# Feed-forward shift and scale as TensorE blocks in the state-space layer, weight remainders there on VectorE, lent buffers returned early

## The chip, the cores and the metric

The kernel runs on one core of one Trainium2 chip. The metric is device time in microseconds (us) of one execution, the median of three runs. In the profile PE is TensorE (PEld its weight loads), DVE is VectorE, ACT is ScalarE, POOL is GpSimd and SP is the queue that issues the DMAs. Each engine works through its own instructions in their order and waits at an instruction until its inputs are there and its output buffer is free.

## The reference, cut to what matters

The whole is four transformer-like layers over 256 tokens of width 1024, in float32. The change lies in one of them, the second layer of the first block: a state-space mixer (S5) with a gate, whose two neighbours are feed-forwards.

```python
def modulation(cs, w, b):
    m = cs @ w + b
    shift, scale, gate = jnp.split(m, 3, axis=-1)
    return shift[:, None, :], scale[:, None, :], gate[:, None, :]

def s5_mixer(h, w_in, ..., w_glu, b_glu, w_out):
    u = h @ w_in
    ...                               # bu = u times B, a scan over time, y = C times the state + d * u
    g = jax.nn.gelu(y)
    z = g * jax.nn.sigmoid(g @ w_glu + b_glu)
    return z @ w_out

    # in layer i, with cs = silu(c), c of shape (1, 1024):
    x = layer_norm(ALPHA * x + (1.0 + gate) * y, ln_mix_g[i], ln_mix_b[i])
    shift, scale, gate = modulation(cs, mod_ffn_w[i], mod_ffn_b[i])
    h = x * (1.0 + scale) + shift
```

A modulation is a product of one row of 1024 with a 1024 x 3072 matrix: little arithmetic, 12 MB of weights. The second feed-forward's shift and scale (`mod30` and `mod31` in the kernel) are needed at the end of the state-space layer.

## The kernel before, in words

All weights come as units of 128 x 1024 float32 (512 KB). `plan()` puts the units into one order, SP loads them in that order into seven buffers `raw`, and `run(maxn)` processes the next units, at most `maxn`, where the program calls it. A buffer is loaded again when its unit has been processed.

A weight unit (`"w"`) is split into a rounded part and a remainder, so that three products of the faster float32r kind give a float32 result. ACT writes the rounded part `wh` (L454). The remainder `wl` is written by DVE in one instruction (L460), or, for the units listed in `POOLED`, by POOL in four of 256 columns (L458). Both go to one of 11 slots (`RING`), and the slot is free again when the matmuls that read it have been issued. Three of the 11 slots (`SPARE`) are lent to the state-space layer, which keeps its operators in them (`self.rt`), so in that layer only eight slots are there for weights: the eight units `ssm_glu` of the gate fill them.

A modulation unit (`"m"`) holds 128 rows of a transposed weight matrix; DVE multiplies it with `cs`, which is spread over the partitions, and sums each row (L508, with a short second instruction that reads the sum). Eight units make the 1024 values of a third (shift, scale or gate), and one small addition of the bias (L517) ends it.

The state-space layer is written by hand as a string of steps, `SSM_SEQ`. Ahead of them stands a pass of the input projection: for each half of the tokens and each of two column blocks n, 8 units of `ssm_in` by three matmuls of 512 columns, with `run` after each unit as `FRUN` says, and a 32 x 32 block transposition on DVE (L1545) after each column block. The last of these passes is the one of half 1, n = 1. In the string the letters with a block number 0 to 3 mean:

- V: enter, 16 float32 matmuls of 64 columns on PE
- R: rotate, four products on DVE (L1571 to L1575), two sums on POOL (L1573, L1576)
- S: scan, two scans and four products on DVE (L1585 to L1591), two sums on POOL (L1589, L1592)
- O: put out, 24 float32 matmuls of 128 columns on PE, then copies by ACT (L1610)
- U: eight transposes on PE (L1620), then the gelu on ACT and DVE, and the split of its result
- G: gates, 48 float32r matmuls of 256 columns on PE; G0 needs all of `ssm_glu`
- X and W expand operators on ACT; a bare number is `run(maxn=number)`

A float32 matmul stands as two records in the trace, each with a weight load of its own. After G3 come the sigmoid by tanh, the split of the gated values into `hh` and `hl` in four blocks of two rows of 128 (L1657 to L1662), with `run(maxn=2)` after each, and then the output projection `ssm_out`: two passes over 8 units, one for each half of the tokens, the first of which needs blocks in their order. The layer norm follows (L651 and on).

What sets the order of work is thus the text of the program: nothing is moved by a scheduler, and each engine's queue is the order in which the steps were called.

Of the kernel before, what the change touches and what calls it, by code (L numbers as in the profile page):

```python
# [15 lines left out]
OP = mybir.AluOpType  # L16
# [16 lines left out]
LATE = {'mla_o': 3, 'mlp0.d': 6, 'ssm_out': 3, 'mlp1.d': 3, 'f10.d': 2, 'lru_out': 2, 'f20.d': 2, 'f11.d': 1, 'att_o': 1, 'f21.d': 3}  # L33
LATE_F = {"mlp0.f": 2, "ssm_in": 2, "mlp1.f": 2, "f10.f": 2, "lru_x": 2, "f20.f": 2, "kv_v": 2, "f11.f": 2, "att_q": 2, "f21.f": 2}
SSM_PRE = 2
SSM_SEQ = "V0 R0 V1 2 X2 0 0 S0 R1 1 V2 X3 W0 4 S1 R2 1 0 2 O0 W1 V3 U0 1 R3 1 S2 1 1 O1 W2 U1 G0 1 S3 W3 O2 1 0 0 0 G1 3 U2 2 O3 U3 0 19 2 1 G2 13 G3"
LRU_SEQ = "X0 X1 C0 X2 C1 Y0 R0 C2 R1 D0 X3 I0 9 I1 C3 Y1 G0 1 G1 7 1 Y2 D1 I2 R2 D2 Y3 I3 R3 G2 G3 D3 A0 1 Q2 3 4 Q1 Q0 6 M0 T0 A1 Q3 M1 A3 3 A2 L0 T1 M2 L1 T2 M3 T3 L2 L3 3 5"
LRU_POOL = {'A0', 'D0', 'D3', 'L2', 'M0', 'M1', 'M2', 'M3', 'N1', 'P0', 'P1', 'P2'}
HEADS0 = "T2 S0 B0 1 A2 E0 N0 t q t 1"
# [42 lines left out]
    return out  # L82


POOLED = {('att_o', 4), ('att_o', 6), ('att_q', 2), ('att_q', 4), ('f20.f', 3), ('f20.f', 6), ('f21.f', 2), ('f21.f', 4), ('f21.f', 7), ('lru_i', 0), ('lru_out', 0), ('lru_out', 1), ('lru_out', 2), ('lru_out', 3), ('lru_out', 4), ('lru_r', 1), ('lru_x', 7), ('lru_y', 2), ('mlp0.f', 3), ('mlp0.f', 4), ('mlp0.f', 5), ('mlp0.f', 7), ('mlp1.f', 1), ('mlp1.f', 2), ('mlp1.f', 3), ('mlp1.f', 4), ('mlp1.f', 5), ('mlp1.f', 6), ('ssm_glu', 1), ('ssm_glu', 2), ('ssm_glu', 3), ('ssm_glu', 4), ('ssm_glu', 5), ('ssm_glu', 6), ('ssm_glu', 7), ('ssm_out', 0), ('ssm_out', 1), ('ssm_out', 2), ('ssm_out', 4)}
LRU_W = _w("lru_x", 8) + _w("lru_y", 2) + [("w", "lru_r", 0), ("w", "lru_i", 0)] + _w("lru_y", 6)[2:]
LRU_W += [("w", "lru_r", 1), ("w", "lru_i", 1)] + _w("lru_y", 8)[6:] + _w("lru_out", 8)
MODS0 = _mod(2, 0) + _mod(2, 1) + _mod(1, 2)
MODS_AT = 8
MODS_PRE = 7  # L90
ON = 1
OM = 4
MM = 3
# [32 lines left out]
def _unit(inp, kind, tag, k, out):  # L126
    def rows(w, cols=slice(0, 1024)):
        out[:] = w[128 * k:128 * k + 128, cols]

    def col(w):  # L130
        out[:] = w[:, 128 * k:128 * k + 128].reshape(8, 128, 128).transpose(1, 0, 2).reshape(128, 1024)

    if kind == "m":
        i, third = int(tag[3]), int(tag[4])
        nm, l = _MOD[i]
        o = 1024 * third + 128 * k
        out[:] = inp[nm + "_w"][l][:, o:o + 128].T
        return
    if tag[:3] in _FFN:
        nm, l = _FFN[tag[:3]]  # L140
        g, u, d = (inp["%s_w_%s_2" % (nm, s)][l] for s in ("gate", "up", "down"))
        part = tag[4]
        if part == "f":
            out[:, :512] = g[128 * k:128 * k + 128, :512]
            out[:, 512:] = u[128 * k:128 * k + 128, :512]
        elif part == "d":
            rows(d)
        else:
            col(g if part == "g" else u)
        return  # L150
    if tag[:3] == "mlp":
        w1, w2 = inp["mlp_w1"][int(tag[3])], inp["mlp_w2"][int(tag[3])]
        if tag[5] == "u":
            col(w1)
        else:
            rows(w1 if tag[5] == "f" else w2)
        return
    if tag == "mla_in":
        w = inp["mla_w_in"][0][256 * k:256 * k + 256].reshape(2, 128, 448)
        out[:, :896] = w.transpose(1, 0, 2).reshape(128, 896)  # L160
    elif tag in ("kvk", "kvv"):
        w = inp["mla_w_kvb"][0].reshape(128, 8, 2, 128)
        out[:] = w[:, :, 0 if tag == "kvk" else 1].reshape(128, 1024)
    elif tag == "qb":
        w = inp["mla_w_qb"][0].reshape(2, 128, 8, 192)[:, :, 2 * k:2 * k + 2]
        o = out.reshape(128, 2, 4, 128)
        for s in range(2):
            o[:, s, 0:2] = w[s, :, :, :128]
            o[:, s, 2] = w[s, :, :, 128:].reshape(128, 128)
            sw = np.concatenate([w[s, :, :, 160:], w[s, :, :, 128:160]], axis=-1)  # L170
            o[:, s, 3] = sw.reshape(128, 128)
    elif tag == "mla_o":
        rows(inp["mla_w_o"][0])
    elif tag == "ssm_in":
        rows(inp["ssm_w_in"][0])
    elif tag == "ssm_glu":
        col(inp["ssm_w_glu"][0])
    elif tag == "ssm_out":
        rows(inp["ssm_w_out"][0])
    elif tag == "lru_x":  # L180
        rows(inp["lru_w_in_2"][0])
    elif tag == "lru_y":
        col(inp["lru_w_in_2"][0][:, 1024:])
    elif tag in ("lru_r", "lru_i"):
        w = inp["lru_w_%s_2" % tag[4]][0][2 * k:2 * k + 2].reshape(2, 2, 128, 256)
        out[:] = w.transpose(2, 0, 1, 3).reshape(128, 1024)
    elif tag == "lru_out":
        rows(inp["lru_w_out_2"][0])
    elif tag == "kv_v":
        rows(inp["w_kv_2"], slice(1024, 2048))  # L190
    elif tag == "kv_k":
        col(inp["w_kv_2"])
    elif tag == "att_q":
        rows(inp["attn_w_q_2"][0])
    elif tag == "att_o":
        rows(inp["attn_w_o_2"][0])
    else:
        raise KeyError(tag)


def _cols_spec():
    s = [("dsk", lambda i: i["ssm_d"][0])]
    for m, (nm, l) in _MOD.items():
        s.append(("modb%d" % m, lambda i, nm=nm, l=l: i[nm + "_b"][l]))
    for nm in ("ln_mix", "ln_ffn"):
        for l in range(2):
            for gb in "gb":
                key = "%s_%s" % (nm, gb)
                s.append((key + str(l), lambda i, key=key, l=l: i[key][l]))
# [12 lines left out]
    return s
# [92 lines left out]
class Model:  # L315
    def __init__(self, ctx, tc, ws, cols, rows, x, pos, inv, rel, sp, sbc, sgb, out):
# [181 lines left out]
    def mod_unit(self, u, raw):  # L498
        nc, tag, k = self.nc, u[1], u[2]
        i, third = int(tag[3]), int(tag[4])  # L500
        if k == 0:
            self.mod_finish()
        total = (self.gcol if tag == "mod01" else self.msum)[:, k:k + 1]
# [421 lines left out]
    def setup(self):  # L925
# [572 lines left out]
    def ssm(self, begin):  # L1498
# [68 lines left out]
        def rotate(b):  # L1567
# [2 lines left out]
            c, sn = tabs[b][:, 0:512], tabs[b][:, 512:1024]  # L1570
            V.tensor_tensor(t[0], vr, c, op=mul)  # L1571
            V.tensor_tensor(t[1], vi, sn, op=mul)
            nc.gpsimd.tensor_tensor(t[0], t[0], t[1], op=add)  # L1573
            V.tensor_tensor(t[2], vi, c, op=mul)
            V.tensor_tensor(t[3], vr, sn, op=mul)  # L1575
            nc.gpsimd.tensor_tensor(t[2], t[2], t[3], op=sub)  # L1576
            self.rel(vr, vi)

        def scan(b):
# [6 lines left out]
            V.tensor_tensor_scan(t[3], mkb, t[2], 0.0, op0=mul, op1=add)  # L1586
            V.tensor_tensor(t[0], t[1], c, op=mul)
            V.tensor_tensor(t[2], t[3], sn, op=mul)
            nc.gpsimd.tensor_tensor(sh(xr)[:, :, 1:64], sh(t[0])[:, :, 0:63], sh(t[2])[:, :, 0:63], op=sub)  # L1589
            V.tensor_tensor(t[1], t[1], sn, op=mul)  # L1590
            V.tensor_tensor(t[3], t[3], c, op=mul)  # L1591
            nc.gpsimd.tensor_tensor(sh(xi)[:, :, 1:64], sh(t[1])[:, :, 0:63], sh(t[3])[:, :, 0:63], op=add)  # L1592
            if b == 0:
                nc.sync.dma_start(out=tabs[3], in_=self.tab_d[3])
            if b == 3:
# [45 lines left out]
                        self.done(u)  # L1641

        for step in SSM_SEQ.split():
            f = {"X": lambda b: expand("g", b), "W": lambda b: expand("h", b), "V": enter, "R": rotate, "S": scan, "O": put_out, "U": unit, "G": gates}.get(step[0])
            if f:
                f(int(step[1:]))
            else:
                self.run(maxn=int(step), mods=99)
        self.rt = []
        self.hidden(1)  # L1650
        bh = self.stat(8)
        V.tensor_scalar(bh, self.col("bglu", 0, 8), 0.5, None, op0=mul)
# [368 lines left out]
```

## Time and profile before

| | |
|---|---|
| median of three runs | 1743.57 us (1743.54 to 1747.07) |
| profiled execution | 1742.75 us, span 1740.9 us |
| PE busy | 1602.5 us (92% of the span) |
| DVE, ACT, POOL busy | 67%, 48%, 29% |
| mean granted TensorE clock | 0.956 of full |

The time of an execution lies 1.85 us above the span of its profile. PE is busy for nearly all of the span; the stretch from about 421 to 505 us, the steps V2 to G3 of the state-space layer, is one of the places where it is not. A share of busy time over the whole span says little of this stretch, so it is read by itself below, with the pass ahead of it (from 400 us) and the gated tail behind it (to 528 us).

### The profile page before, as it was taken

Reading aid. Unit: us, or ns where it says so; the run is one execution under the profiler, and the core shown is the slowest. Engines: PE = TensorE matmul, PEld = TensorE weight load, DVE = VectorE, ACT = ScalarE, POOL = GpSimd, SP = SyncE. Lnnn points to the kernel's source line nnn. Section 1 sums busy time; section 2 is a strip of 40 time slices with the busy share of each in tenths; the row PEclk is TensorE's granted clock in tenths of the full one; section 3 lists DMA queues with packets and bytes.
Section 4 is the critical chain, followed back from the end, with each engine's and each line's share of the span. In section 5 each row is a group of like instructions: output and inputs, shape, how many; then the busy total and the mean of one; then the engine's idle time right before and its main releaser. Section 6 shows DMA issues by size and latency. Waiting matters only on the chain. (4 is left out here: it accounts for less than half of the span.)

```text
span 1740.9 us, 25278 instructions
## 1 busy us (share of the span) xinstructions
PE 1602.5 (92%) x9690; PEld 1417.2 (81%) x9690; DVE 1157.7 (67%) x1480; ACT 833.7 (48%) x1252; POOL 508.8 (29%) x557
## 2 busy tenths in 40 slices
PE   4778999998789999999999759999999999999998
PEld 2557798887677899789998747999899999779997
DVE  6688986578978655776556787555656554765553
ACT  2343656555345655354445735444544443754441
POOL 8945699608848100100004441000000001230000
PEclk9869999898889999999999879999999999999999
DMA  9477678767556666466554336565455664536640
GB/s 365 172 279 256 226 248 281 273 243 263 220 170 222 239 229 212 152 219 225 176 181 134 118 121 217 176 239 173 137 188 214 213 211 133 182 133 207 214 149 25
DMA packets 106588, 349.64 MB, mean 201 GB/s; under 512 B 12385, under 2 KB 22753, under 8 KB 106466
## 3 DMA queue, kind: packets, MB, share of 16 engines
q1 hardware_dynamic: 106466, 348.02, 57.7%
q8 instruction: 76, 1.25, 0.3%
q14 instruction: 46, 0.38, 0.1%
HBM read 338.40 MB, written 9.57 MB: 200 GB/s over the span
## 5 line engine op out<-in xcount | busy, mean ns | idle before, releaser
L460 DVE TENSOR_TENSOR wl<-raw,wh 128x1024 fp32r<-128x1024 f32 x445 | 562.7, 1298 | 193.1 <-ACT wh L454 191.7
L454 ACT ACTIVATE wh<-raw 128x1024 fp32r<-128x1024 f32 x484 | 490.3, 1051 | 275.1 <-PE bank L392 140.9
L392 PE MATMUL bank<-xh,wh 128*128 128x256 f32 x1728 | 490.1, 284 | 0.0
L392 PE MATMUL bank<-xh,wl 128*128 128x256 f32 x1728 | 489.7, 283 | 0.0
L392 PE MATMUL bank<-xl,wh 128*128 128x256 f32 x1728 | 489.1, 283 | 0.0
L392 PEld LDWEIGHTS bank<-xh,wh 128*128 128x128 f32 x1728 | 330.6, 191 | 2.4 <-issue 0.2
L392 PEld LDWEIGHTS bank<-xl,wh 128*128 128x128 f32 x1728 | 330.5, 191 | 2.1
L392 PEld LDWEIGHTS bank<-xh,wl 128*128 128x128 f32 x1728 | 330.5, 191 | 0.0
L392 PE MATMUL bank<-wh,hh 128*128 128x512 f32 x736 | 297.4, 404 | 24.8 <-ACT hh L1827 23.8
L392 PE MATMUL bank<-wl,hh 128*128 128x512 f32 x736 | 294.5, 400 | 2.8 <-POOL wl L458 2.8
L392 PE MATMUL bank<-wh,hl 128*128 128x512 f32 x736 | 244.8, 398 | 4.2 <-DVE hl L590 2.0
L635 POOL TENSOR_TENSOR st<-st,mhalf 128x1 f32<-128x1 f32 (+1 forms) x33 | 21.9, 664 | 694.8 <-DVE st L643 608.1
L458 POOL TENSOR_TENSOR wl<-raw,wh 128x256 fp32r<-128x256 f32 x156 | 156.7, 1037 | 138.0 <-ACT wh L454 129.8
L392 PEld LDWEIGHTS bank<-wh,hh 128*128 128x128 f32 x736 | 142.0, 193 | 55.9 <-ACT hh L1827 25.3
L392 PEld LDWEIGHTS bank<-wh,hl 128*128 128x128 f32 x736 | 141.1, 192 | 37.5 <-DVE hl L590 2.9
L392 PEld LDWEIGHTS bank<-wl,hh 128*128 128x128 f32 x736 | 142.2, 193 | 33.1 <-POOL wl L458 5.0
L508 DVE SCALAR_TENSOR_TENSOR junk<-raw,cs 128x1024 bf16<-128x1024 f32 x96 | 138.0, 1437 | 18.3 <-DMA raw<-in_ws_dram 17.1
L392 PE MATMUL bank<-wl,xh 128*128 128x512 f32 x320 | 126.6, 396 | 1.9 <-DVE wl L460 1.0
L392 PE MATMUL bank<-wh,xh 128*128 128x512 f32 x320 | 127.4, 398 | 0.7 <-ACT wh L454 0.7
L590 DVE TENSOR_TENSOR hl<-z,hh 128x512 fp32r<-128x512 f32 x72 | 52.5, 731 | 95.5 <-ACT hh L589 95.3
L392 PE MATMUL bank<-wh,xl 128*128 128x512 f32 x320 | 102.0, 396 | 6.5 <-DVE xl L590 6.4
L589 ACT ACTIVATE hh<-z 128x512 fp32r<-128x512 f32 x72 | 45.5, 632 | 116.4 <-DVE z L875 104.4
(389 smaller groups left out, 1807.2 us busy)
## 6 DMA issues: line engine op xcount, KB each, us to landing
raw<-in_ws_dram SPq DMA_DIRECT2D x580, 512.0 KB
early<-in_ws_dram SPq DMA_DIRECT2D x10, 512.0 KB
grow<-in_rows_dram SPq DMA_DIRECT2D x9, 512.0 KB
brow<-in_rows_dram SPq DMA_DIRECT2D x6, 512.0 KB
ophh<-ops_d SPq DMA_DIRECT2D x6, 512.0 KB
ophl<-ops_d SPq DMA_DIRECT2D x6, 512.0 KB
gate<-in_rows_dram SPq DMA_DIRECT2D x5, 512.0 KB
tab_d<-early SPq DMA_DIRECT2D x4, 512.0 KB
```

The lines of the kernel that those rows point to most:

```text
L392: self.nc.tensor.matmul(out, l, r, start=start, stop=stop)
L454: self.nc.scalar.activation(self.Hs[s], raw, func=AF.Copy)
L458: self.nc.gpsimd.tensor_tensor(self.Ls[s][:, w], raw[:, w], self.f32(self.Hs[s])[:, w], op=OP.subtract)
L460: self.nc.vector.tensor_tensor(self.Ls[s], raw, self.f32(self.Hs[s]), op=OP.subtract)
L508: nc.vector.scalar_tensor_tensor(self.junk, raw, 1.0, self.cs, op0=OP.mult, op1=OP.mult, accum_out=total)
L589: self.nc.scalar.activation(hdst, src, func=AF.Copy)
L590: self.nc.vector.tensor_tensor(ldst, src, self.f32(hdst), op=OP.subtract)
L635: self.nc.gpsimd.tensor_tensor(r, v, self.mhalf[:, 0:n], op=OP.pow)
```

## The change

1. The 16 units of `mod30` and `mod31` (`ROWMODS`) are laid out as plain rows of the weight matrix. Instead of the DVE product, `pe_unit` issues eight float32 matmuls: a 128 x 128 piece of the unit is the stationary operand, one column of `cst` (the 1024 values of `cs`, laid over 128 partitions and 8 columns) is what moves, and the result is one column of a PSUM bank. All eight units add into eight columns of one bank, which is held from the first to the last; then DVE adds the bias, reading from PSUM.
2. `cst` is made at the start: one ACT and two DVE instructions on 128 x 8 values.
3. Seven units of `ssm_glu` and `ssm_out` 0, 1 and 2 leave `POOLED`: DVE writes their remainders.
4. A step Z empties `self.rt` after O3, so the three lent slots are open to weights; `SSM_W` brings `ssm_out` 0 to 2 ahead of the last two units of `mod22`, and `SSM_SEQ` processes them before G2.
5. The sums of R and S on POOL are each written in two halves.

```diff
-SSM_SEQ = "... G1 3 U2 2 O3 U3 0 19 2 1 G2 13 G3"
+SSM_SEQ = "... G1 3 U2 2 O3 Z0 U3 0 3 G2 13 G3"
-POOLED = {..., ('ssm_glu', 1), ..., ('ssm_glu', 7), ('ssm_out', 0), ('ssm_out', 1), ('ssm_out', 2), ('ssm_out', 4)}
+POOLED = {..., ('ssm_out', 4)}
+ROWMODS = {'mod30', 'mod31'}
-SSM_W = _w('ssm_glu', 8)[:4] + _mod(3, 0) + _w('ssm_glu', 8)[4:] + _mod(3, 1) + _mod(2, 2) + _w('ssm_out', 8)
+SSM_W = _w('ssm_glu', 8)[:4] + _mod(3, 0) + _w('ssm_glu', 8)[4:] + _mod(3, 1) + _mod(2, 2)[:6] + _w('ssm_out', 8)[:3]
+SSM_W += _mod(2, 2)[6:] + _w('ssm_out', 8)[3:]
...
+    def pe_unit(self, tag, k, raw):
+        nc = self.nc
+        if k == 0:
+            self.pbk = self.bank()
+        for j in range(8):
+            self.mm(self.pbk[:, j:j + 1], raw[:, 128 * j:128 * j + 128], self.cst[:, k:k + 1],
+                    k == 0 and j == 0, k == 7 and j == 7)
+        if k == 7:
+            i, third = int(tag[3]), int(tag[4])
+            dst = self.mcol[i][third] if third < 2 else self.gcol
+            nc.vector.tensor_tensor(dst, self.pbk[:, 0:8], self.col("modb%d" % i, 8 * third, 8), op=OP.add)
+            self.rel(self.pbk)
+            self.pbk = None
...
+        ct = self.col("c", 0, 8)
+        nc.scalar.activation(self.cst, ct, func=AF.Tanh, scale=0.5)
+        V.scalar_tensor_tensor(self.cst, self.cst, 1.0, ct, op0=OP.add, op1=OP.mult)
+        V.tensor_scalar(self.cst, self.cst, 0.5, None, op0=OP.mult)
...
-            nc.gpsimd.tensor_tensor(t[0], t[0], t[1], op=add)
+            for w in (slice(0, 256), slice(256, 512)):
+                nc.gpsimd.tensor_tensor(t[0][:, w], t[0][:, w], t[1][:, w], op=add)
...
-        self.rt = []
```

How the queues move. First PE, in the last pass of the input projection (half 1, n = 1), around its fifth unit; `wh` and `wl` are a unit's two parts, `xh` and `xl` those of the input. Before:

```order
L392 MATMUL bank_124<-wh_59_928,xl 128x512
L392 MATMUL bank_124<-wh_60_933,xh 128x512
L392 MATMUL bank_124<-wl_60_934,xh 128x512
L392 MATMUL bank_124<-wh_60_933,xl 128x512
L392 MATMUL bank_124<-wh_50_797,xh 128x512
L392 MATMUL bank_124<-wl_50_798,xh 128x512
L392 MATMUL bank_124<-wh_50_797,xl 128x512
L392 MATMUL bank_124<-wh_51_811,xh 128x512
```

and now:

```order
L399 MATMUL bank_125<-wh_59_932,xl 128x512
L399 MATMUL bank_129<-cst,raw_64 128x1 x8
L399 MATMUL bank_125<-wh_60_937,xh 128x512
L399 MATMUL bank_125<-wl_60_938,xh 128x512
L399 MATMUL bank_125<-wh_60_937,xl 128x512
L399 MATMUL bank_125<-wh_50_801,xh 128x512
L399 MATMUL bank_125<-wl_50_802,xh 128x512
L399 MATMUL bank_125<-wh_50_801,xl 128x512
L399 MATMUL bank_129<-cst,raw_65 128x1 x8
L399 MATMUL bank_129<-cst,raw_66 128x1 x8
L399 MATMUL bank_125<-wh_51_815,xh 128x512
```

Three modulation units stand between the units of the pass here, and a fourth before its last unit. Then PE where V1 ends and V2 begins (`z` is the projected input, `oph` and `opl` are expanded operators). Before:

```order
L392 MATMUL bank_125<-z_99,oph_2876 128x64
L392 MATMUL bank_126<-z_99,opl_2877 128x64
L392 MATMUL bank_131<-z_99,oph_2878 128x64
L392 MATMUL bank_127<-z_99,opl_2879 128x64
L392 MATMUL bank_131<-z_99,oph_2878 128x64
```

and now:

```order
L399 MATMUL bank_127<-z_99,oph_2880 128x64
L399 MATMUL bank_132<-z_99,opl_2881 128x64
L399 MATMUL bank_129<-cst,raw_68 128x1 x8
L399 MATMUL bank_129<-cst,raw_69 128x1 x8
L399 MATMUL bank_129<-cst,raw_63 128x1 x8
L399 MATMUL bank_128<-z_99,oph_2882 128x64
L399 MATMUL bank_130<-z_99,opl_2883 128x64
L399 MATMUL bank_128<-z_99,oph_2882 128x64
```

Three units stand between V1 and V2; three more follow V2, four U0, one G0 and one O2. Last DVE from the end of R1 to the start of S1 (`mc` is the finished shift, `grow` holds the rotation's table). Before:

```order
L1575 TENSOR_TENSOR z_98<-bank_125,grow 128x512
L508 SCALAR_TENSOR_TENSOR junk,msum<-raw_63,cs 128x1024
L508 SCALAR_TENSOR_TENSOR junk,msum<-raw_64,cs 128x1024
L517 TENSOR_TENSOR mc_115<-msum,cols 128x8
L1585 SCALAR_TENSOR_TENSOR z_98<-z_100,z_98 128x512
```

and now:

```order
L1610 TENSOR_TENSOR z_98<-bank_127,grow 128x512
L545 TENSOR_TENSOR mc_115<-bank_129,cols 128x8
L467 TENSOR_TENSOR wl_60_938<-raw_65,wh_60_937 128x1024
L467 TENSOR_TENSOR wl_50_802<-raw_66,wh_50_801 128x1024
L467 TENSOR_TENSOR wl_51_816<-raw_67,wh_51_815 128x1024
L1621 SCALAR_TENSOR_TENSOR z_98<-z_100,z_98 128x512
```

Two modulation products have gone from between R1 and S1, three remainders have come, and the addition of the bias now reads the PSUM bank that PE fills.

## Rows read from the trace of the kernel before

**Rows 1.** Busy time of each engine by stretch; PEclk is the granted clock.

```profile
core 0: us, PE busy (x) PEld busy (x) DVE busy (x) ACT busy (x) POOL busy (x), PEclk, DMA share, GB/s
421.20:505.35 84.15, 65.97 (x481) 62.40 (x481) 76.52 (x98) 28.37 (x56) 48.21 (x39) 0.82 0.62 221
505.35:528.26 22.91, 17.99 (x66) 13.22 (x65) 14.91 (x16) 15.91 (x23) 18.36 (x20) 0.78 0.52 179
```

**Rows 2.** Waits of PE, 421.20 to 505.35 us: total, times, longest.

```profile
PE bank L392 <- POOL ophh L1589: 7.8, 1, 7.8
PE bank L1620 <- ACT b2row L1610: 2.3, 2, 1.9
```

**Rows 3.** DVE by line, 408.6 to 503.1 us: count, busy us, mean ns.

```profile
L508 DVE SCALAR_TENSOR_TENSOR junk<-raw,cs 128x1024 bf16<-128x1024 f32 x24 | 36.1, 1504 | 3.8 <-DMA raw<-in_ws_dram 3.4
```

**Rows 4.** The page's costliest groups: DVE's remainders over the whole span.

```profile
L460 DVE TENSOR_TENSOR wl<-raw,wh 128x1024 fp32r<-128x1024 f32 x445 | 562.7, 1298 | 193.1 <-ACT wh L454 191.7
```

**Rows 5.** PE in time order (start, length): last pass, V0, V1, V2.

```profile
406.62 0.39 PE L392 MATMUL bank<-wh,xh 128*128 128x512 f32 x1
...
412.14 0.33 PE L392 MATMUL bank<-z,oph 128*128 128x64 f32 x2
...
419.01 0.39 PE L392 MATMUL bank<-z,opl 128*128 128x64 f32 x2
421.20 0.66 PE L392 MATMUL bank<-z,oph 128*128 128x64 f32 x2 [1.80 <-DVE z L1545]
...
427.62 0.64 PE L392 MATMUL bank<-z,opl 128*128 128x64 f32 x2
```

**Rows 6.** DVE in time order: the fourth modulation unit and the last transposition.

```profile
418.68 1.73 DVE L508 SCALAR_TENSOR_TENSOR junk<-raw,cs 128x1024 bf16<-128x1024 f32 x1 [3.36 <-DMA raw<-in_ws_dram]
...
420.35 0.70 DVE L1545 STREAM_TRANSPOSE z<-bank 128x512 f32<-128x512 f32 x1
```

**Rows 7.** PE in time order: first and last row of O at full clock.

```profile
485.51 0.43 PE L392 MATMUL bank<-ophl,z 128*64 128x128 f32 x2
...
490.62 0.38 PE L392 MATMUL bank<-opl,ophl 128*64 128x128 f32 x2
```

**Rows 8.** Busy time by stretch: V2 and idling, most of O0, G0.

```profile
421.20:434.66 13.46, 8.84 (x38) 7.92 (x39) 13.43 (x18) 4.17 (x7) 8.23 (x12) 0.50 0.80 292
434.66:438.36 3.70, 3.70 (x19) 3.70 (x19) 3.67 (x4) 0.97 (x2) 3.70 (x3) 0.52 0.78 282
...
462.96:468.70 5.74, 5.74 (x48) 5.69 (x48) 5.74 (x5) 3.17 (x8) 5.05 (x4) 1.00 0.74 276
```

**Rows 9.** PE in time order: a matmul of 32 columns, and what follows it.

```profile
259.63 0.31 PE L392 MATMUL bank<-z 128*128 128x32 f32 x2
259.78 0.69 PE L392 MATMUL bank<-z,b2row 128*128 128x128 f32 x4
```

**Rows 10.** Weight loads (PEld) in time order at that place.

```profile
259.52 0.30 PEld L392 LDWEIGHTS bank<-z 128*128 128x128 f32 x2
259.75 0.53 PEld L392 LDWEIGHTS bank<-z,b2row 128*128 128x128 f32 x4
```

**Rows 11.** PE in time order: tail, with 512-column matmuls at half clock.

```profile
511.69 0.63 PE L392 MATMUL bank<-wh,hh 128*128 128x512 f32 x1
512.12 0.65 PE L392 MATMUL bank<-wl,hh 128*128 128x512 f32 x1
```

**Rows 12.** Waits of PE, 505.35 to 530 us: total, times, longest.

```profile
PE bank L392 <- POOL wl L458: 2.8, 3, 1.1
```

**Rows 13.** Busy time by stretch: the tail after its waits on POOL.

```profile
519.00:523.00 4.00, 4.00 (x11) 3.13 (x10) 3.31 (x4) 2.82 (x4) 3.58 (x4) 0.50 0.69 254
```

**Rows 14.** ACT in time order: the last block of the gated values.

```profile
520.18 0.63 ACT L1661 ACTIVATE hh<-z 128x512 fp32r<-128x512 f32 x1 [2.08 <-DVE z L1658]
```

**Rows 15.** DVE in time order: a small operation, and the layer norm's start.

```profile
502.63 0.17 DVE L520 TENSOR_TENSOR gcol<-msum,cols 128x8 f32<-128x8 f32 x1
...
528.23 0.69 DVE L651 TENSOR_TENSOR r<-bank,gate 128x512 f32<-128x512 f32 x1 [1.94 <-PE bank L392]
```

More of the change, by code (lines that the diff above doesn't have):

```diff
@@ L35 @@
 SSM_PRE = 2
-SSM_SEQ = "V0 R0 V1 2 X2 0 0 S0 R1 1 V2 X3 W0 4 S1 R2 1 0 2 O0 W1 V3 U0 1 R3 1 S2 1 1 O1 W2 U1 G0 1 S3 W3 O2 1 0 0 0 G1 3 U2 2 O3 U3 0 19 2 1 G2 13 G3"
+SSM_SEQ = "V0 R0 V1 2 X2 0 0 S0 R1 1 V2 X3 W0 4 S1 R2 1 0 2 O0 W1 V3 U0 1 R3 1 S2 1 1 O1 W2 U1 G0 1 S3 W3 O2 1 0 0 0 G1 3 U2 2 O3 Z0 U3 0 3 G2 13 G3"
 LRU_SEQ = "X0 X1 C0 X2 C1 Y0 R0 C2 R1 D0 X3 I0 9 I1 C3 Y1 G0 1 G1 7 1 Y2 D1 I2 R2 D2 Y3 I3 R3 G2 G3 D3 A0 1 Q2 3 4 Q1 Q0 6 M0 T0 A1 Q3 M1 A3 3 A2 L0 T1 M2 L1 T2 M3 T3 L2 L3 3 5"
@@ L82, in _weave @@
     return out
-POOLED = {('att_o', 4), ('att_o', 6), ('att_q', 2), ('att_q', 4), ('f20.f', 3), ('f20.f', 6), ('f21.f', 2), ('f21.f', 4), ('f21.f', 7), ('lru_i', 0), ('lru_out', 0), ('lru_out', 1), ('lru_out', 2), ('lru_out', 3), ('lru_out', 4), ('lru_r', 1), ('lru_x', 7), ('lru_y', 2), ('mlp0.f', 3), ('mlp0.f', 4), ('mlp0.f', 5), ('mlp0.f', 7), ('mlp1.f', 1), ('mlp1.f', 2), ('mlp1.f', 3), ('mlp1.f', 4), ('mlp1.f', 5), ('mlp1.f', 6), ('ssm_glu', 1), ('ssm_glu', 2), ('ssm_glu', 3), ('ssm_glu', 4), ('ssm_glu', 5), ('ssm_glu', 6), ('ssm_glu', 7), ('ssm_out', 0), ('ssm_out', 1), ('ssm_out', 2), ('ssm_out', 4)}
+POOLED = {('att_o', 4), ('att_o', 6), ('att_q', 2), ('att_q', 4), ('f20.f', 3), ('f20.f', 6), ('f21.f', 2), ('f21.f', 4), ('f21.f', 7), ('lru_i', 0), ('lru_out', 0), ('lru_out', 1), ('lru_out', 2), ('lru_out', 3), ('lru_out', 4), ('lru_r', 1), ('lru_x', 7), ('lru_y', 2), ('mlp0.f', 3), ('mlp0.f', 4), ('mlp0.f', 5), ('mlp0.f', 7), ('mlp1.f', 1), ('mlp1.f', 2), ('mlp1.f', 3), ('mlp1.f', 4), ('mlp1.f', 5), ('mlp1.f', 6), ('ssm_out', 4)}
 LRU_W = _w("lru_x", 8) + _w("lru_y", 2) + [("w", "lru_r", 0), ("w", "lru_i", 0)] + _w("lru_y", 6)[2:]
@@ L135, in _unit @@
         nm, l = _MOD[i]
+        if tag in ROWMODS:
+            rows(inp[nm + "_w"][l], slice(1024 * third, 1024 * third + 1024))
+            return
         o = 1024 * third + 128 * k
@@ L201, in _cols_spec @@
 def _cols_spec():
-    s = [("dsk", lambda i: i["ssm_d"][0])]
+    s = [("dsk", lambda i: i["ssm_d"][0]), ("c", lambda i: i["c"][0])]
     for m, (nm, l) in _MOD.items():
@@ L347, in __init__ @@
         self.mhalf = T("mhalf", [128, 4])
+        self.cst = T("cst", [128, 8])
+        self.pbk = None
         self.lri = T("lri", [128, 8], I32)
@@ L500, in mod_unit @@
         i, third = int(tag[3]), int(tag[4])
+        if tag in ROWMODS:
+            self.pe_unit(tag, k, raw)
+            return
         if k == 0:
@@ L521, in mod_unit @@
                 nc.vector.tensor_scalar(self.gcol, self.gcol, 1.0, None, op0=OP.add)
+                self.modfin = [tag, 3]
+    def pe_unit(self, tag, k, raw):
[10 more added lines that the diff above has]
+            self.rel(self.pbk)
+            self.pbk = None
+            if third < 2:
+                self.mods.add(tag)
+            else:
+                nc.vector.tensor_scalar(dst, dst, 1.0, None, op0=OP.add)
                 self.modfin = [tag, 3]
@@ L1572, in rotate @@
             V.tensor_tensor(t[1], vi, sn, op=mul)
-            nc.gpsimd.tensor_tensor(t[0], t[0], t[1], op=add)
+            for w in (slice(0, 256), slice(256, 512)):
+                nc.gpsimd.tensor_tensor(t[0][:, w], t[0][:, w], t[1][:, w], op=add)
             V.tensor_tensor(t[2], vi, c, op=mul)
             V.tensor_tensor(t[3], vr, sn, op=mul)
-            nc.gpsimd.tensor_tensor(t[2], t[2], t[3], op=sub)
+            for w in (slice(0, 256), slice(256, 512)):
+                nc.gpsimd.tensor_tensor(t[2][:, w], t[2][:, w], t[3][:, w], op=sub)
             self.rel(vr, vi)
@@ L1588, in scan @@
             V.tensor_tensor(t[2], t[3], sn, op=mul)
-            nc.gpsimd.tensor_tensor(sh(xr)[:, :, 1:64], sh(t[0])[:, :, 0:63], sh(t[2])[:, :, 0:63], op=sub)
+            for q in (slice(0, 4), slice(4, 8)):
+                nc.gpsimd.tensor_tensor(sh(xr)[:, q, 1:64], sh(t[0])[:, q, 0:63], sh(t[2])[:, q, 0:63], op=sub)
             V.tensor_tensor(t[1], t[1], sn, op=mul)
             V.tensor_tensor(t[3], t[3], c, op=mul)
-            nc.gpsimd.tensor_tensor(sh(xi)[:, :, 1:64], sh(t[1])[:, :, 0:63], sh(t[3])[:, :, 0:63], op=add)
+            for q in (slice(0, 4), slice(4, 8)):
+                nc.gpsimd.tensor_tensor(sh(xi)[:, q, 1:64], sh(t[1])[:, q, 0:63], sh(t[3])[:, q, 0:63], op=add)
             if b == 0:
@@ L1643, in ssm @@
         for step in SSM_SEQ.split():
-            f = {"X": lambda b: expand("g", b), "W": lambda b: expand("h", b), "V": enter, "R": rotate, "S": scan, "O": put_out, "U": unit, "G": gates}.get(step[0])
+            f = {"X": lambda b: expand("g", b), "W": lambda b: expand("h", b), "V": enter, "R": rotate, "Z": lambda b: self.rt.clear(), "S": scan, "O": put_out, "U": unit, "G": gates}.get(step[0])
             if f:
```

## The prediction

> **What bounds the kernel now.** The share of busy time says PE nearly everywhere, so I read the windows by stretch first. From 421.20 to 505.35 us (V2 to the end of G3) PE is busy 65.97 of 84.15 us, 18.2 idle, at a granted clock of 0.82, while DVE is busy for 76.52 [rows 1]. The list of waits says who stood in the way: PE waited 7.8 us, once, for POOL's sum of a scan, which stood in POOL's queue behind weight remainders, and 2.3 us for ACT ahead of U [rows 2]. DVE's groups by line then say what fills DVE: 24 modulation products, 36.1 us in all, 1.504 each [rows 3]. So the stretch ends when DVE and POOL let it, and PE has some 18 us to spare. The tail to the layer norm takes 22.91 us with PE busy for 17.99 [rows 1]; there PE waits 2.8 us, in three times, for POOL's remainders [rows 12], and the 4 us behind these waits run at 0.50 [rows 13].
>
> One thing in these rows matters more than the idling. V0 and V1, 62 records of 64-column matmuls, ran from 412.14 to 419.01 at one pace, 0.111 us per record ((419.01 - 412.14)/62 = 0.1108) [rows 5]. Then PE waited 1.80 us for the transposition, and V2, the same instructions, ran from 421.20 to 427.62 in 15 pairs, 0.428 a pair, 0.214 per record: the clock had gone to 1.2 GHz [rows 5]. The stretch up to 434.66 has 0.50, and O0 behind it still has 0.52 up to 438.36, with PE busy all of its 3.70 us [rows 8]. So V2's unbroken stream of narrow matmuls did not bring 2.4 GHz back; some 3.7 us of O's 128-column matmuls did.
>
> **The change: what leaves.** Sixteen products leave DVE: 16 x (1.504 + 0.08 for the short read of the sum, about half of a small operation's 0.17 [rows 15]) = 25.3 us [rows 3]. Ten remainders come from POOL: 10 x 1.298 = 13.0 us [rows 4]. Net -12.3 for DVE, of 76.52; POOL loses 40 quarter remainders, so the wait of 7.8 has no cause left. With 64 of 84 us, DVE is not the bound any more if PE's queue is no shorter than before. The halved POOL sums cost one more start each, on an engine that is now mostly free: nothing.
>
> **What comes to PE.** A unit is eight float32 matmuls, so 16 records, each with its own 128-column weight load, and one column that moves. No row shows a one-column matmul. The nearest rows are the 64-column ones: 0.111 us per record at full clock [rows 5]. O, with 128 columns, has (490.62 - 485.51)/46 = 0.111 as well [rows 7], so it is not the columns that set this pace, but the load; I take 16 x 0.111 = 1.78 us at full clock and 16 x 0.214 = 3.41 at half, 1.63 more. The lower end is the 32-column place: 0.15 us from the pair to what follows it, 0.075 per record [rows 9], so 1.16 us a unit, though the loads there stand 0.23 apart for a pair [rows 10], again near 0.11. The upper end is a fifth more than mine, 0.13 per load, as the four loads there ran [rows 10].
>
> The Trainium skill ("TensorE: Matmul & The Clock Gate", section "LDWEIGHTS (loading the stationary operand)") puts a load at its columns divided by 1.2 GHz, 107 ns for 128, and names no dependence on the granted clock. At full clock the trace agrees (0.111), at half it doesn't (0.214). By that rule a unit would cost 1.71 us at either clock; what this gives is rival C.
>
> **At full clock.** From 406.62, the first row taken of the last pass, to 505.35 are 98.7 us before. PE's own work there: pass 5.5 (406.62 to 412.14 [rows 5]), four V at 32 x 0.111 = 3.56, four O at 48 x 0.111 = 5.3, four U 2.6 (eight transposes each, estimated at 0.08), four G at 5.74 [rows 8]: 66.5 us. Sixteen units add 28.5, together 95.0. Add two waits that stay: m3 (units are m0 to m15) stands before the last unit of the pass and its data land at 418.68 [rows 6], 1.9 us after PE would be there; and U's 2.3 [rows 2]. That is 99.2, or +0.5 against before. So even undisturbed PE merely swaps idling for loads: 18.2 idle, 28.5 added.
>
> **The clock.** A string of three units is 48 loads with one column each, 5.3 us of a stream far narrower than V2's, which did not hold the chip at 2.4 GHz. I therefore let the clock fall in the strings m1 to m3, m4 to m6, m7 to m9 and m10 to m13, and come back only after the 3.7 us of O that rows 8 show. What runs at 1.2 GHz then costs: m1 to m3 +4.9; two triples of 512-column matmuls in the pass at 0.43 each ([rows 11], half of that at full clock), +1.3 less rounding, 1.2; the wait for m3 vanishes, -1.9; V0, V1 and V2 between the strings, 3 x 3.27 = +9.8 (32 x 0.102); m4 to m9 +9.8; the first part of O0, +2.0; m12 and m13 +3.3; the first part of O1 +2.0. Sum +31.1, so G3 ends at 505.35 + 0.5 + 31.1 = 537, +31.5. V3, U0, m14 and m15, which stand alone between dense steps, are taken at full clock.
>
> **Waits that the change adds.** DVE's bias addition now waits for m7; behind it three remainders and S1 are queued. From m7 to O1, which needs S1, PE has m8, m9, O0, V3, U0, m10 to m13: about 28 us. DVE needs 3 x 1.30 and six instructions of 0.7 to 1.3 us [rows 4, 6], at most 12, and POOL two sums. Covered; were it not, O1 would wait the difference. SP's loads of the 16 raws now wait for PE rather than DVE: as PE is behind, buffers come free later, and weights arrive later by as much as PE is late, which by itself adds nothing, since PE asks for them later too.
>
> **Start and tail.** The three small operations for `cst` at the start cost at least 0.17 each [rows 15], 0.5 in all; I take 0.4, since part lies beside waits (0 to 0.6). In the tail `ssm_out` 0 to 2 are ready and DVE has no more to do, so the waits for POOL, 2.8 [rows 12], go, and so does most of the half clock behind them, 1.7 of the 2.0 that 4 us at 0.50 hold [rows 13]: -4.5. Against it: the first pass needs the four blocks of gated values, and the last `hh` is written at 520.18 after 2.08 of waiting for DVE [rows 14], with no POOL in that chain; ends are therefore -1 and -6.5. What is late next is PE itself: the layer norm already waits 1.94 for it [rows 15].
>
> **Sum.** +31.5 - 4.5 + 0.4 = +27.4. On the profiled execution's 1742.75 (its span and 1.85 around it) this is 1770.2; the median of the runs lies 0.8 above that execution, so 1771.
>
> **The rivals.**
> A, the other side: the clock holds. If a load counts as work, or the stretches of units are too short to matter, the sum is +0.5 - 4.5 + 0.4 = -3.6, so 1740. It decides at one point: the granted clock in the first string, m4 to m6. For it: V0 and V1 kept 2.4 GHz over 6.9 us with 64 columns a load [rows 5]. Against: V2's stream, with loads just as dense, did not win it back [rows 8].
> B, the clock falls only inside the long strings and dense work wins it back at once: m4 to m13 (10 x 1.63 = 16.3) and V2 between two strings (3.3), so +16.0 in all, 1760. Against it: 3.70 us of O0 at 0.52 [rows 8].
> C, units cost the same at either clock, only other steps are slowed: without the 18.0 for m1 to m9, m12 and m13, +9.4, 1753. Against it stands V2's 0.214 per record [rows 5].
> D, units are cheap and the clock holds: at 1.16 us [rows 9] 9.9 less than A, 1730. The Trainium skill (same page, section "Back-to-back issue gap") gives about 25 ns as the least distance of small matmuls; were loads hidden, a unit would be 0.4 us by it, and 16 units would take 22 less than in A, an estimate from that page of 1718. The 64-column rows at 0.111 [rows 5] speak against both.
> E, half clock nearly throughout, O, V3, m14 and m15 included: +17.2 + 3.3 + 3.3, 1795, and more if G0 and G1 are slowed. Against it: G0 ran at 1.00 behind such work [rows 8].
> That the change doesn't do what it says (the slots lent back early bring `ssm_out` forward, and the tail is paced by the gated values anyway) takes the 4.5 away: 1775, inside my range.
>
> **How the numbers follow.** Chances: forecast 0.56, A 0.14, B 0.11, C 0.05, D 0.09, E 0.05. The forecast's own range: V0 and V1 at full clock (-6.5), a better tail (-2) and less of O (-3) give 1759; a tail without gain (+3.5), m14, m15 and half of G0 slowed (+6) give 1780; dearer loads a little more. To hold 8 in 10 the range reaches down to A, leaving out D and some of A below, E and a little of the forecast above: 1738 to 1783. A measurement of this kernel tells about 0.2%, 3.5 us, from no change, and A lies just there: half of A and D are faster, 0.16; half of A is the same, 0.07; the rest is slower, 0.77.
>
> **What would show it.** In the changed kernel's trace: records on `cst` 0.11 apart would be A, 0.21 the forecast, under 0.08 D; the windows should show 0.5 from m1 to the middle of O0 and again in m12 to O1; no PE wait for POOL's sums; G3's end near 537; DVE idle before the bias addition, waiting for PE; the tail from G3 to the layer norm near 18 us. The forecast is wrong at its root if V0 to V2 run at 0.111 a record behind the units, and wrong in size if only O's first part or the tail differs.

## The result, and the profile after

The changed kernel takes 1770.37 us (median of 4 runs, 1766.23 to 1772.37) against 1744.28 before (now four runs, 1743.54 to 1747.07): a ratio of 1.0144, 95% interval 1.0121 to 1.0166, slower by about 26 us. The profiled execution took 1766.23, 23.5 more than that of before. The ratios of the experiments leave out two executions at a far lower clock, one of the kernel before (2153 us at 0.68) and one of the changed kernel with its units back on DVE (1984 us at 0.75).

The stretch that [rows 1] and [rows 8] show for before looks like this now, as busy time by stretch (columns as in [rows 1]; the granted clock is the number behind the five engines):

```profile
core 0: us, PE busy (x) PEld busy (x) DVE busy (x) ACT busy (x) POOL busy (x), PEclk, DMA share, GB/s
419.01:439.23 20.22, 18.80 (x85) 18.11 (x84) 6.78 (x9) 3.65 (x7) 3.70 (x4) 0.52 0.49 200
439.23:466.57 27.34, 27.34 (x129) 27.33 (x129) 11.40 (x15) 6.73 (x11) 6.28 (x8) 0.50 0.57 196
466.57:478.40 11.83, 11.83 (x90) 11.52 (x89) 5.19 (x8) 4.37 (x10) 7.38 (x8) 0.82 0.53 198
478.40:497.50 19.10, 19.10 (x114) 18.95 (x112) 10.82 (x13) 2.96 (x5) 8.09 (x8) 0.64 0.46 148
497.50:537.86 40.36, 39.66 (x345) 38.61 (x344) 24.57 (x36) 18.05 (x34) 3.49 (x4) 1.00 0.42 139
537.86:557.50 19.64, 15.57 (x64) 12.89 (x63) 12.78 (x19) 14.09 (x22) 5.83 (x7) 0.83 0.74 251
```

DVE, busy for 76.5 of 84 us before, is busy for 34 of the 78 us between 419 and 497.5, and PE for 77. PE's only gap there is one of 1.42 us, and from 419 to 466.6 it works at 0.50 to 0.52. The places behind this, in the changed kernel's PE in time order (start, length, operation, count):

```profile
411.79 1.84 PE L399 MATMUL bank<-cst,raw 128*128 128x1 f32 x16
...
414.98 3.63 PE L399 MATMUL bank<-cst,raw 128*128 128x1 f32 x32
...
420.83 3.57 PE L399 MATMUL bank<-cst,raw 128*128 128x1 f32 x16 [1.42 <-DMA raw<-in_ws_dram]
...
425.69 0.52 PE L399 MATMUL bank<-z,oph 128*128 128x64 f32 x2
...
456.30 10.35 PE L399 MATMUL bank<-cst,raw 128*128 128x1 f32 x48
466.57 0.69 PE L399 MATMUL bank<-ophl,z 128*64 128x128 f32 x2
...
470.89 0.38 PE L399 MATMUL bank<-oph,z 128*64 128x128 f32 x2
...
478.40 11.37 PE L399 MATMUL bank<-cst,raw 128*128 128x1 f32 x64
489.69 0.69 PE L399 MATMUL bank<-ophl,z 128*64 128x128 f32 x2
```

These rows answer [rows 5] and [rows 7]. At full clock m0, and m1 with m2, take 1.7 to 1.8 us a unit for 16 records, about 0.11 each. At half clock m7 to m9 take (466.57 - 456.30)/48 = 0.214 us a record. V0 and V1, 0.111 a record before, run at 0.21 now, as V2 did already before. O0's pairs stand 0.43 apart up to 470.46 and 0.22 from 470.89 on: the clock comes back 4.3 us into O0, and is lost again in m10 to m13 (64 records in 11.3 us). Nothing stands between U0 and m10, so no wait of PE lowered the clock there. G3 ends at 537.9, against 505.4.

DVE now waits for PE, as its waits from 406 to 570 us show (total, times, longest):

```profile
DVE mc L545 <- PE bank L399: 18.9, 2, 15.9
```

and the longer one, at the addition of the bias:

```profile
459.85 0.17 DVE L545 TENSOR_TENSOR mc<-bank,cols 128x8 f32<-128x8 f32 x1 [15.94 <-PE bank L399]
```

It costs PE nothing: S1's products are done at 468, POOL's sums of them at 470.7, and O1, which needs them, starts on PE at 489.69. The waits of PE for POOL's sum [rows 2] and for POOL's remainders in the tail [rows 12] are gone. What PE waits for in the tail now (537.86 to 560 us) is the tanh of the gated values, 4.1 us for 2.1 before:

```profile
PE bank L399 <- ACT z L1694: 4.1, 2, 2.9
```

### The profile page after: what moved, and what is told of

Same layout as the page of the kernel before. It is cut to its first block, busy times and chain, and to the rows that moved or that the text cites. A ratio compares the mean times of both kernels' runs of the same rounds, so it can differ in the third digit from the quotient of the medians.

```text
span 1764.4 us, 25743 instructions
## 1 busy us (share of the span) xinstructions
PE 1634.7 (93%) x9946; PEld 1453.8 (82%) x9946; DVE 1132.8 (64%) x1460; ACT 834.2 (47%) x1253; POOL 466.5 (26%) x533
## 5 line engine op out<-in xcount | busy, mean ns | idle before, releaser
L467 DVE TENSOR_TENSOR wl<-raw,wh 128x1024 fp32r<-128x1024 f32 x455 | 570.6, 1289 | 190.6 <-ACT wh L461 189.3
L465 POOL TENSOR_TENSOR wl<-raw,wh 128x256 fp32r<-128x256 f32 x116 | 112.1, 1000 | 150.9 <-ACT wh L461 150.2
L518 DVE SCALAR_TENSOR_TENSOR junk<-raw,cs 128x1024 bf16<-128x1024 f32 x80 | 111.3, 1392 | 17.0 <-DMA raw<-in_ws_dram 16.2
```

What stands on the lines that cost most here:

```text
L465: self.nc.gpsimd.tensor_tensor(self.Ls[s][:, w], raw[:, w], self.f32(self.Hs[s])[:, w], op=OP.subtract)
L467: self.nc.vector.tensor_tensor(self.Ls[s], raw, self.f32(self.Hs[s]), op=OP.subtract)
L518: nc.vector.scalar_tensor_tensor(self.junk, raw, 1.0, self.cs, op0=OP.mult, op1=OP.mult, accum_out=total)
```

## The experiments

Two theories stood against each other: the clock (narrow strings of units take PE to 1.2 GHz, and everything up to O then runs at half speed), and the records alone (16 weight loads a unit cost their time, whatever the clock). A third, that the moved remainders and the new order delay, was tested by undoing the units alone. A fourth lies close to the first: that it is PE's wait for m3, and not the strings, that lowers the clock; the traces of the experiments decide it. Each ratio is to the kernel before in runs of the same batch (medians 1744.05 to 1746.81).

| kernel | median, us | ratio to before, 95% interval |
|---|---|---|
| changed | 1770.37 | 1.0144 (1.0121 to 1.0166) |
| units back on DVE | 1737.02 | 0.9963 (0.9945 to 0.9980) |
| the same again | 1737.88 | 0.9956 (0.9940 to 0.9972) |
| before + units on PE only | 1773.74 | 1.0170 (1.0154 to 1.0186) |
| 128 columns a matmul | 1739.57 | 0.9969 (0.9956 to 0.9982) |
| 64 columns a matmul | 1736 to 1747, or 1762 to 1765 | see below |
| `mod31` alone, 128 columns | 1738.68 | 0.9966 (0.9954 to 0.9979) |
| `mod30` alone, 128 columns | 1737.84 | 0.9956 (0.9942 to 0.9970) |
| `mod31` alone, one column | 1747.38 | 1.0013 (0.9999 to 1.0027) |
| tail's part undone | 1773.23 | 1.0161 (1.0144 to 1.0177) |
| before + `ssm_glu` remainders on DVE | 1744.77 | 0.9994 (0.9978 to 1.0009) |
| before + tail's part | 1742.47 | 0.9985 (0.9972 to 0.9997) |

**Units back on DVE.**

```diff
-ROWMODS = {'mod30', 'mod31'}
+ROWMODS = set()
```

> The changed kernel with all 16 units as DVE products again (ROWMODS empty); the remainders on VectorE, the early return of the lent buffers and the halved sums stay. Theory (the units on PE, by the clock they take away, are the whole loss): 1740 to 1757; DVE has about 13 us more than before in a stretch where it was busy 76.5 of 84 us, so a small loss may be left, but G3 ends by 520 at the latest against 537.9, and V2 to G3 has a granted clock near 0.8. Rival 1 (the units cost PE's time by their number of records, whatever the clock): the same here. Rival 2 (the moved remainders and the changed order are what delays): 1760 or more.

The whole loss is gone, and the rest of the change is left as a small gain, 1737.02. Busy time over the stretch of [rows 1]:

```profile
core 0: us, PE busy (x) PEld busy (x) DVE busy (x) ACT busy (x) POOL busy (x), PEclk, DMA share, GB/s
421.20:505.35 84.15, 66.06 (x493) 61.86 (x492) 77.33 (x103) 34.00 (x64) 38.08 (x32) 0.84 0.64 228
```

and what PE waited for there (421 to 507 us):

```profile
PE bank L399 <- POOL z L1626: 6.9, 2, 4.0
PE bank L399 <- POOL z L1630: 3.2, 2, 2.1
PE bank L399 <- POOL ophh L1626: 2.8, 1, 2.8
```

This is before's picture, PE 66 of 84 us and DVE 77, with PE's wait for the sums split over more of them. So rival 2, the other parts, is out.

**Units on PE and nothing else.** The kernel before, with `ROWMODS`, `pe_unit` and `cst` added.

> The kernel before with the 16 units on PE and nothing else changed (remainders on POOL, lent buffers held, sums whole). Theory: the strings of units lower the clock as in the changed kernel, G3 ends at 535 to 545, and the total is 1768 to 1780, since the tail keeps POOL's remainders (about 3 us more than in the changed kernel). Rival 1 (records, not clock): also about 1770. Rival 2: the loss comes from the other parts, so this one is near 1744.

1773.74, with G3's end at 537.0. The stretch from 421 to 440 us shows the same clock with no part of the change but the units:

```profile
core 0: us, PE busy (x) PEld busy (x) DVE busy (x) ACT busy (x) POOL busy (x), PEclk, DMA share, GB/s
421.00:440.00 19.00, 19.00 (x88) 18.71 (x87) 8.16 (x10) 4.33 (x9) 3.14 (x9) 0.50 0.47 169
```

Its PE shows more. m1 and m2, and what follows them:

```profile
415.26 4.53 PE L398 MATMUL bank<-cst,raw 128*128 128x1 f32 x32
419.65 0.77 PE L398 MATMUL bank<-wh,xh 128*128 128x512 f32 x1
```

Here PE waits for no load at all, and the clock falls inside m1 and m2: 32 records in 4.39 us, where the changed kernel took 3.49. So the string lowers it without a wait.

Neither of these two runs tells the clock from the records. The next does.

**128 columns a matmul.** The same records and weight loads; the column is moved 128 times over, into two banks.

```diff
...
-            self.mm(self.pbk[:, j:j + 1], raw[:, 128 * j:128 * j + 128], self.cst[:, k:k + 1],
-                    k == 0 and j == 0, k == 7 and j == 7)
+            o = 128 * (j % 4)
+            self.mm(self.pbk[j // 4][:, o:o + 128], raw[:, 128 * j:128 * j + 128],
+                    self.cst[:, k:k + 1].to_broadcast([128, 128]), k == 0 and j % 4 == 0, k == 7 and j % 4 == 3)
...
```

> The changed kernel, but each of a unit's matmuls moves 128 equal columns of cst instead of one; the same number of records and weight loads, 128 times the columns, and one bank more. Theory (clock): 128-column matmuls brought 2.4 GHz back in O0, so the strings now hold it; a record stays at 0.11 us as in O, V0 to V2 run at 0.111 a record, G3 ends at 506 to 510 against 537.9, total 1737 to 1746. Rival 1 (the units cost by their records and weight loads, and DVE's wait for the bias addition sets the rest): no gain, 1766 to 1772, or longer for the more columns.

More work on PE, and 31 us less: 1739.57. Its busy time by stretch, and m3 and two strings of units in PE's order:

```profile
core 0: us, PE busy (x) PEld busy (x) DVE busy (x) ACT busy (x) POOL busy (x), PEclk, DMA share, GB/s
421.80:448.40 26.60, 25.18 (x217) 24.39 (x215) 15.23 (x21) 10.17 (x17) 9.97 (x12) 1.00 0.81 306
448.40:465.40 17.00, 17.00 (x153) 16.65 (x152) 13.44 (x19) 6.74 (x14) 9.19 (x11) 1.00 0.73 282
465.40:511.30 45.90, 45.19 (x394) 43.82 (x392) 30.45 (x43) 18.66 (x35) 9.82 (x10) 1.00 0.47 161
```

```profile
424.14 2.05 PE L399 MATMUL bank<-cst,raw 128*128 128x128 f32 x16 [1.42 <-DMA raw<-in_ws_dram]
...
433.82 5.58 PE L399 MATMUL bank<-cst,raw 128*128 128x128 f32 x48
439.24 0.33 PE L399 MATMUL bank<-z,oph 128*128 128x64 f32 x2
...
442.76 5.71 PE L399 MATMUL bank<-cst,raw 128*128 128x128 f32 x48
448.40 0.43 PE L399 MATMUL bank<-ophl,z 128*64 128x128 f32 x2
```

The clock is 1.00 from 421.8 to 511.3, the 48 records of three units take 5.4 to 5.6 us instead of 10.3, V2 takes 3.5 instead of 6.9, and G3 ends at 511.3. That is 1.3 behind the range expected, but the lateness stood ahead of the stretch: from m0 (before, the fifth unit of the pass, at 409.37) to G3's end it took 96.0 us before, 126.1 in the changed kernel and 96.2 here. A record costs 0.113 to 0.117 us with 128 columns and 0.106 to 0.109 with one at the same clock, so the number of columns hardly sets the pace. The wait for m3 is 1.42 us here too, and the clock stays at 1.00 behind it. The records alone, and the wait alone, are refuted as the cause; that it is the narrow columns that lose the clock here is shown.

**64 columns a matmul.** As above, with `[128, 64]`, in one bank.

> As the run with 128 columns, but 64 equal columns a matmul, in one bank. Theory (clock): V0 and V1 kept 2.4 GHz with 64 columns a load, V2 did not win it back; so if the pass leaves the clock high it stays high through m4 to V2 and the total is 1738 to 1750; where a wait of PE lowers it once, the strings behind do not bring it back and the total lies between 1750 and 1768. Rival 1: 1766 to 1772 as with one column.

Both branches of the expectation came true, in different executions: its ten times form two groups, five from 1736.0 to 1747.4 at mean clocks of 0.964 to 0.969, and five from 1762.3 to 1765.4 at 0.952 to 0.955. The profiled one is of the first group and shows where the edge is. PE in time order, and the busy time by stretch around that place:

```profile
442.21 3.74 PE L399 MATMUL bank<-cst,raw 128*128 128x64 f32 x32
446.96 3.32 PE L399 MATMUL bank<-cst,raw 128*128 128x64 f32 x16 [1.01 <-DMA raw<-in_ws_dram]
```

```profile
core 0: us, PE busy (x) PEld busy (x) DVE busy (x) ACT busy (x) POOL busy (x), PEclk, DMA share, GB/s
421.80:446.90 25.10, 23.19 (x199) 22.44 (x198) 14.17 (x19) 10.17 (x17) 9.97 (x12) 1.00 0.80 300
446.90:450.20 3.30, 3.24 (x16) 3.13 (x16) 3.30 (x4) 0.00 (x0) 0.00 (x0) 0.57 0.99 387
450.20:457.60 7.40, 7.40 (x50) 7.22 (x49) 5.92 (x9) 0.59 (x1) 6.25 (x7) 0.73 0.37 146
```

The first stretch holds a wait of 0.95 us ahead of m3, with 512-column matmuls on both sides, and kept 2.4 GHz; so did the 19.8 us of 64-column matmuls from V0 to m8 (426.19 to 445.95). Behind the wait of 1.01 us for m9's load the clock was lost, and m9 and part of O0 paid for it (3.3 us for 1.8, and 7.3 for 5.4). That the second group loses it earlier, ahead of m4, would fit its 20 us, but no execution of that group was profiled.

**Half of the units.** `ROWMODS = {'mod31'}` and `{'mod30'}` with 128 columns, and `{'mod31'}` with one.

> Only the eight units of mod31 on PE, with 128 equal columns each; mod30 stays on DVE as before, the other parts as in the changed kernel. Theory (PE has room for loads only up to its idling, and wide strings keep the clock): with all units on DVE PE idled 23 us of 400 to 520; eight units of 1.78 to 1.9 us are 15, and DVE loses 12.7, so G3 ends at 496 to 506 and the total is 1728 to 1738, less than with none (1737) or all sixteen (1740). Rival (DVE's products are covered by other waits, so moving them gains nothing): 1736 to 1742.

> The eight units of mod30 on PE instead, 128 equal columns each; mod31 on DVE. Theory: the same amounts of work, but four of these units stand ahead of or between V0 to V2, where PE waits least for DVE, and DVE's S1 waits for m7: 1730 to 1740, not better than with mod31. Rival: no difference to none, 1736 to 1742.

> The eight units of mod31 on PE with one column each, as the changed kernel has them; mod30 on DVE. Theory (clock): m8 and m9, and above all the string m10 to m13, lower the clock again; half the units at up to 3.4 us each and V or O behind them at half clock cost 8 to 20 us against the wide ones: 1740 to 1755. If it was the number of loads alone that cost the time, it equals the wide ones within 2 us.

With eight units less on PE I expected up to 9 us more than the 1737 with none there; `mod31` alone gives 1738.68, just outside, and `mod30` alone 1737.84, no better than none. PE's waits in the first of them (406 to 530 us) show one thing that ate the gain:

```profile
PE bank L399 <- DMA raw<-in_ws_dram: 7.3, 2, 4.2
```

m8 and m9 stand in PE's queue ahead of O0, and now PE waits for their weights, 7.3 us; all 24 products on DVE had waited 3.4 us for loads [rows 3]. The clock had fallen ahead of them, behind a wait of 2.0 us between V1 and V2, and m8 and m9 ran at half of it even with 128 columns. With `mod30` alone there is no such wait, and no experiment shows what held that kernel back.

With one column the same eight units cost 8.7 us more than with 128 (1747.38 against 1738.68, and the intervals of the ratios lie apart), as the clock theory wants. The two profiles can't price this difference, since they happen to take the same time (1742.00, the shortest of ten, and 1742.08, the longest of eight). They do show where the columns tell. With 128 columns, m8, m9, and m10 to m13:

```profile
437.02 3.78 PE L399 MATMUL bank<-cst,raw 128*128 128x128 f32 x16 [3.02 <-DMA raw<-in_ws_dram]
...
445.05 3.78 PE L399 MATMUL bank<-cst,raw 128*128 128x128 f32 x16 [4.25 <-DMA raw<-in_ws_dram]
...
459.57 7.41 PE L399 MATMUL bank<-cst,raw 128*128 128x128 f32 x64
```

and m10 to m13 with one:

```profile
453.72 11.84 PE L399 MATMUL bank<-cst,raw 128*128 128x1 f32 x64
```

m8 and m9 are slow in both, 3.78 us here and 3.57 with one column, behind waits of 3.9 and 4.4 us. The string m10 to m13, with no wait ahead of it, takes 7.4 us in one and 11.8 in the other.

**The tail and the remainders.** The lent buffers held to G3 again, with `ssm_out` 0 to 2 late and on POOL:

> The changed kernel with the tail's part undone: the lent buffers go back after G3, ssm_out 0 to 2 come behind mod22 and their remainders are on POOL again; the units stay on PE. Theory: G3's end does not move by more than 2 us (537.9), and from there to the layer norm the tail is 2 to 4 us longer, as POOL's remainders are waited for again; total 1770 to 1776. Rival: the blocks of gated values pace the tail, so nothing changes, 1768 to 1772.

From G3's end to the layer norm's first statistics it takes 24.2 us instead of the changed kernel's 21.7 (by the medians the whole is 2.9 longer, with intervals that overlap), and PE (539 to 565 us) waits again for what [rows 12] showed:

```profile
PE bank L398 <- POOL wl L464: 4.1, 5, 1.1
```

The two parts alone, on the kernel before:

> The kernel before with nothing changed but the remainders of ssm_glu 1 to 7, written by DVE instead of POOL. Theory: PE's wait of 7.8 us for POOL's sum goes, but DVE gets 9.1 us more in a stretch where it was busy 76.5 of 84 us; so G3 ends within 4 us of before's 505.4 and the total is 1740 to 1748. Rival (POOL's backlog alone was the bound): G3 6 to 8 us earlier, 1736 to 1738.

> The kernel before with the tail's part alone: lent buffers back after O3, ssm_out 0 to 2 brought ahead of the last two units of mod22 and processed before G2, their remainders on DVE. Theory: from G3's end to the layer norm 2 to 4 us less than before, as taking it out of the changed kernel cost 2.4 there; total 1738 to 1743, with G3's end within 2 us of before. Rival: DVE, the bound ahead of G3, takes the three remainders' 3.9 us there, and nothing is left: 1743 to 1746.

> The changed kernel with the units as DVE products, once more, for its interval beside the two parts alone: 1733 to 1740. If the gains of the two parts add up, their sum is this one's 7 us against before; if they do not, moving remainders and the tail's order help only together (POOL free and weights early).

The `ssm_glu` remainders on DVE alone change nothing that can be told from zero: PE's wait of 7.8 us for POOL's sum [rows 2] is down to 2.5, but G3 ends 3 us later than before. The tail's part alone is worth 0.15% (0.03 to 0.28), with 21.8 us from G3 to those statistics against 24.9 before. Both together, with the halved sums, give 0.44% (0.28 to 0.60). By their middles the parts alone make half of that; the intervals are too wide to say whether the rest is the two helping each other or the halved sums, which were not run alone. The version with the units on DVE beats both kernels, and no version with units on PE can be told to be faster than it.

## Why the prediction was right

It was right in sign and in mechanism, narrow units taking PE to half clock, and close in size: 1771 forecast, 1770.4 measured. That the two lie within a microsecond is in part luck, since errors of up to 5.8 us cancel. By its steps, for the profiled execution:

- **Price of a unit.** 0.111 us a record at full clock and 0.214 at half were forecast from V0 to V2 [rows 5]; 0.106 to 0.109 and 0.214 were measured. The one-column matmul costs what the 64-column one does.
- **Where the clock falls.** V0 to V2 (+9.8 forecast, 13.54 + 6.86 - 3 x 3.56 = +9.7 measured) and m4 to m9 (+9.8, and 10.2 + 10.3 - 6 x 1.78 = +9.8) were exact. O0 cost +2.2 for 2.0, O1 +2.5 for 2.0, m10 to m13 +4.2 for 3.3: the clock came back a little later, and fell earlier, than taken.
- **Wrong in the pass.** m1 and m2 ran at 0.109 a record: two units in a row, between triples of 512-column matmuls, did not lower the clock in this execution; it fell around PE's wait for m3, which did not vanish (1.42 left, 0.5 won of 1.9). m1 to m3 cost 1.6 rather than 4.9, and one triple, not two, was slowed. That makes the pass 3.8 cheaper than forecast by the clock and 1.4 dearer by the wait. In the kernel with the units alone, and in the one with the tail undone, the clock did fall in m1 and m2 (32 records in 4.39 and 4.26 us), so the place differs between executions.
- **G3's end.** 537.9 against 537. Of that shift, 2.4 us were there already ahead of the stretch, so the stretch itself gave 30.1 for 31.5. U's waits for ACT, 2.3 in the sum, were 0.7.
- **The tail.** From G3's end to the layer norm 22.9 became 558.05 - 537.86 = 20.2, so -2.7 and not -4.5. The waits for POOL went, as forecast, but PE then waited 4.1 us for the gated values instead of 2.1, and the half clock behind a wait stayed (0.83 in the tail's window): the objection with [rows 14] held in part.
- **The start.** +0.4 forecast, and +2.4 ahead of the stretch (the first row of the last pass at 409.05 for 406.62). The first layer norm's statistics start at 144.0 in the profile of before, at 143.6 to 146.6 in the ten profiles with `cst`, and at 145.7 and 145.8 in the two experiments without it, so the profiles put no price on the three operations.
- **Behind the layer norm** the code is the same, and this execution was 5.8 us faster there than that of before (from 530.27 to the span's end 1210.6 us, and now 1204.8). The forecast set nothing there. The steps add up to 2.4 + 30.1 - 2.7 - 5.8 = 24.0, near the 23.5 by which the profiles differ, for 27.4 forecast; the medians differ by 26.1.

Rival A was worth writing down: its price for the same units at full clock, 1740, is what the kernel with 128 columns measured (1739.57), and its +0.5 from the pass to G3's end was +0.2 there. B, C, D and E fell with the rows above: O0 needs 4.3 us to get the clock back, units cost twice at half clock, no record at `cst` takes under 0.1 us, and the clock is 1.00 from 497.5 to 537.86. (In D, 16 records of 0.075 are 1.20 us, not 1.16; the rival becomes 1731.)

## What to carry to other kernels

Before moving small products to an engine with idle time, ask what pace and what clock the new stream has there: here 18 us of PE's idling were filled by 28 us of weight loads with almost nothing behind them, and the lost clock doubled V0, V1 and parts of O0 and O1 besides. Where such a stream must be on TensorE, more columns a load can keep the clock at almost no cost (128 here, at most 0.01 us a record more), as long as PE isn't kept waiting between them, as it was for m8 and m9; single units between dense work, m0, m14 and m15, ran at full clock too, 1.7 to 1.8 us each. But a kept clock is not yet a gain: with it, the units on PE were no faster than on DVE. A wait for a load moves with the instruction: with `mod31` alone PE waited 7.3 us for weights that stood in its queue ahead of other work.

## What the runs showed of the hardware

- Strings of weight loads with one moving column each took the granted clock from 1.00 down with no wait of PE: 64 records of 128 x 128 weights (m10 to m13) in the changed kernel, 32 (m1 and m2) in the kernel with the units alone. Two strings of 48 and the 64-column V0 to V2 between them then stayed at 0.50. With 128 columns the same loads stayed at 1.00. PE and PEld were busy nearly 100% in both.
- Columns alone don't settle it where PE waits. Between units of 128 columns the clock stayed at 1.00 behind a wait of 1.42 us; with `mod31` alone, where it had fallen at a wait of 2.0 us between V1 and V2, single 128-column units behind waits of 3.0 and 4.3 us ran at 0.50, 3.7 us each.
- With 64 columns the clock was kept for 19.8 us without a wait, and lost behind a wait of 1.01 us. The executions of that kernel form two groups of times, 20 us apart, of which one was profiled.
- Unchanged code from the state-space layer's norm to the end differed by 5.8 us between two profiled executions of different kernels, so a few microseconds in one profile are no verdict on a change.
